# Rotary embedding on half of each head: cosine and sine rows landed on every fourth partition and gathered on VectorE

## The chip, the cores and the metric

The kernel runs on one core of one Trainium2 chip. The metric is the device time of the core in microseconds (us), lower is better; medians of several executions are given. All runs quoted here are at full granted clock. Profiles are of one execution; "span" is its length.

## The reference

```python
# x: 16 x 512 x 16 x 64 fp32;  cos, sin: 512 x 32 fp32
x1, x2 = x[..., :32], x[..., 32:]
a, b = x1[..., :16], x1[..., 16:]            # c, s: the first 16 columns of cos, sin by position
first  = a * c - b * s
second = a * s + b * c
out = concatenate([first, second, x2])       # 33.6 MB in, 33.6 MB out
```

## The kernel before

The 8192 positions are cut into four tiles of 128 partitions with 16 positions each (K = 16). Partition p of every tile needs rows 16(p mod 32) to 16(p mod 32)+15 of the tables, so a table of 32 partitions is replicated four times (REP = 4, PB = 32, Q = 16, HF = 32). A ring holds three tiles; each is loaded, rotated in place by VectorE and stored.

```python
ring  = const_pool.tile([P, NS, K, H, D], fp32)        # NS = 3
stage = const_pool.tile([PB, 2, K, HF], fp32)
table = const_pool.tile([P, 2, K, 2, Q], fp32)

nc.gpsimd.dma_start(out=stage[:, 0]..., in_=cosf)      # 64 KB each, issued by POOL
nc.gpsimd.dma_start(out=stage[:, 1]..., in_=sinf)
load(0, 0, K0); load(0, K0, K); load(1); load(2, 0, KC)  # issued by SP; K0 = 4, KC = 8
for r in range(REP):
    nc.vector.tensor_copy(out=table[r * PB : (r + 1) * PB]..., in_=stage[..., 0:Q] broadcast)

rotate(0, 0, K0); rotate(0, K0, 10); rotate(0, 10, K)  # four VectorE operations each
store(0)                                               # issued by SP too
load(2, KC, K)
load(3)                                                # needs tile 0's slot: waits for store(0)
for t in range(1, T):
    rotate(t, 0, KC); rotate(t, KC, K); store(t)
```

Of the kernel before, what the change touches and what calls it, by code (L numbers as in the profile page):

```python
# [1 line left out]

# [4 lines left out]


@with_exitstack
def kernel(  # L10
    ctx: ExitStack,
    tc: tile.TileContext,
    x: bass.AP,
    cos: bass.AP,
    sin: bass.AP,
    out: bass.AP,
):
    nc = tc.nc
    fp32 = mybir.dt.float32
    P = 128  # L20
    B, S, H, D = x.shape
    Q = D // 4
    HF = D // 2



    K = 16
    T = B * S // (P * K)
    PB = S // K
    REP = P // PB  # L30
    R = H * D
    NS = 3
    KC = K // 2
    K0 = K // 4

    xf = x.rearrange("b s h d -> (b s h d)").rearrange("(t p f) -> t p f", t=T, p=P)
    of = out.rearrange("b s h d -> (b s h d)").rearrange("(t p f) -> t p f", t=T, p=P)
    cosf = cos.rearrange("(p k) j -> p (k j)", k=K)
    sinf = sin.rearrange("(p k) j -> p (k j)", k=K)

    const_pool = ctx.enter_context(tc.tile_pool(name="const", bufs=1))
    b_pool = ctx.enter_context(tc.tile_pool(name="bp", bufs=1, space=bass.MemoryType.PSUM))


    ring = const_pool.tile([P, NS, K, H, D], fp32)
    stage = const_pool.tile([PB, 2, K, HF], fp32)
    table = const_pool.tile([P, 2, K, 2, Q], fp32)

    def rows(t, lo, hi):
        return ring[:, t % NS, lo:hi].rearrange("p k h d -> p (k h d)")  # L50

    def load(t, lo=0, hi=K):
        nc.sync.dma_start(out=rows(t, lo, hi), in_=xf[t, :, lo * R : hi * R])  # L53

    def store(t, lo=0, hi=K):
        nc.sync.dma_start(out=of[t, :, lo * R : hi * R], in_=rows(t, lo, hi))

    nc.gpsimd.dma_start(out=stage[:, 0].rearrange("p k j -> p (k j)"), in_=cosf)  # L58
    nc.gpsimd.dma_start(out=stage[:, 1].rearrange("p k j -> p (k j)"), in_=sinf)  # L59
    load(0, 0, K0)  # L60
    load(0, K0, K)
    load(1)
    load(2, 0, KC)


    for r in range(REP):
        nc.vector.tensor_copy(  # L67
            out=table[r * PB : (r + 1) * PB].rearrange("p t k c j -> p (t k) c j"),
            in_=stage.rearrange("p t k j -> p (t k) j")[:, :, 0:Q]
            .unsqueeze(2)  # L70
            .to_broadcast((PB, 2 * K, 2, Q)),
        )
    C = table[:, 0].rearrange("p k c j -> p k (c j)")
    Sn = table[:, 1].rearrange("p k c j -> p k (c j)")

    def rotate(t, lo, hi):
        n = hi - lo
        x1 = ring[:, t % NS, lo:hi, :, 0:HF]
        c = C[:, lo:hi].unsqueeze(2).to_broadcast((P, n, H, HF))
        s = Sn[:, lo:hi].unsqueeze(2).to_broadcast((P, n, H, HF))  # L80
        b_full = b_pool.tile([P, KC, H, HF], fp32, name="b_t")
        b_t = b_full[:, 0:n]
        nc.vector.tensor_mul(out=b_t, in0=x1, in1=s)  # L83
        nc.vector.tensor_mul(out=x1, in0=x1, in1=c)  # L84
        nc.vector.tensor_sub(  # L85
            out=x1[:, :, :, 0:Q], in0=x1[:, :, :, 0:Q], in1=b_t[:, :, :, Q:HF]
        )
        nc.vector.tensor_add(  # L88
            out=x1[:, :, :, Q:HF], in0=x1[:, :, :, Q:HF], in1=b_t[:, :, :, 0:Q]
        )  # L90

    rotate(0, 0, K0)
    rotate(0, K0, (K0 + K) // 2)
    rotate(0, (K0 + K) // 2, K)
    store(0)
    load(2, KC, K)
    load(3)
    for t in range(1, T):
        rotate(t, 0, KC)
        rotate(t, KC, K)  # L100
        store(t)


# [1 line left out]
_INS = ['x', 'cos', 'sin']  # L105
_OUTS = [((16, 512, 16, 64), 'float32')]


# [23 lines left out]
```

## Time and profile before

| | before |
|---|---|
| time | 161.92 us median of 6 (161.79 to 162.01) |
| span of the profiled run | 160.1 us |
| VectorE busy | 110.0 us, 69% |
| moved by DMA | 67.24 MB, 420 GB/s over the span |
| first rotation starts, second starts | 11.94 us, 23.66 us |
| first store issued | 44.14 us |

The prediction shows the slices, the stretches and the start of the timeline. One more view is needed later: three lines of the chain of waits of the kernel before. The columns are start, length, and what the chain went through.

```profile
1.17 22.39 DMA ring<-in_x_dram
...
44.14 28.18 DMA out_dram<-ring
72.34 28.75 DMA ring<-in_x_dram
```

These are the load of tile 0 (issued, until the whole tile is in), the store of tile 0, and the load of tile 3 into its slot. A transfer's length here is queueing and moving together: 28.18 us is not what 8.4 MB need (at the 433 GB/s of the middle stretches 19.4 us, an estimate), but what lay ahead of them in the queue as well. Between the load and the store the chain runs through VectorE's rotation of tile 0, 20.58 us here and in the changed kernel.

### The profile page before, as it was taken

To read this page: it belongs to the slowest core of one execution; us is meant where nothing else is said; L and a number is where in the kernel's file an instruction comes from. 1 tells how busy PE (TensorE), PEld (TensorE's weight loads), DVE (VectorE), ACT (ScalarE), POOL (GpSimd) and SP (SyncE) were. 2 spreads that over 40 slices of the span, in tenths; PEclk is the share of its full clock that TensorE was granted. 3 is DMA by queue.
4 is the path that set the end of the run, shared out by engine and by line. 5 is a ranking of instruction groups with operands and counts; after the bars stand their busy time and mean duration, and the time that the engine had idled before them with its cause. 6 is when DMAs were issued, how large, how long until landed. Compare 5 with 4: busy or idle time off the path is not lost.

```text
span 160.1 us, 109 instructions
## 1 busy us (share of the span) xinstructions
DVE 110.0 (69%) x40; POOL 1.3 (1%) x6
## 2 busy tenths in 40 slices
DVE  0069709999999999999999994799999900000000
POOL 3000000000000000000000000000000000000000
DMA  6999999699699799899996996996996996996991
GB/s 197 385 504 454 393 459 524 262 524 491 295 401 581 328 524 409 377 393 418 483 540 295 491 524 262 524 524 262 524 524 262 524 524 262 524 491 295 524 459 66
DMA packets 1504, 67.24 MB, mean 420 GB/s; under 512 B 192, under 2 KB 192, under 8 KB 224
## 3 DMA queue, kind: packets, MB, share of 16 engines
q1 hardware_dynamic: 1440, 67.11, 97.8%
q0 software_dynamic: 64, 0.13, 0.2%
HBM read 33.69 MB, written 33.55 MB: 420 GB/s over the span
## 4 chain that ended last, share of the span: by engine, by line
DMA 50%; DVE 28%; DVEq 1%; issue 0%; SPq 0%
DMA ring<-in_x_dram 32%; DMA out_dram<-ring 18%; DVE b_t L83 10%; DVE ring L84 10%; DVE ring L85 5%; DVE ring L88 3%; DVEq L127 1%; SPq L53 0%; DVEq L83 0%
## 5 line engine op out<-in xcount | busy, mean ns | idle before, releaser
L83 DVE TENSOR_TENSOR b_t<-ring,table 128x4096 f32<-128x4096 f32 (+2 forms) x9 | 35.6, 3959 | 8.2 <-DMA ring<-in_x_dram 8.0
L84 DVE TENSOR_TENSOR ring<-ring,table 128x4096 f32<-128x4096 f32 (+2 forms) x9 | 35.6, 3950 | 0.3
L85 DVE TENSOR_TENSOR ring<-ring,b_t 128x2048 f32<-128x2048 f32 (+2 forms) x9 | 18.4, 2049 | 0.3
L88 DVE TENSOR_TENSOR ring<-ring,b_t 128x2048 f32<-128x2048 f32 (+2 forms) x9 | 18.4, 2042 | 0.0
L67 DVE COPY table<-stage 32x1024 f32<-32x1024 f32 x4 | 2.7, 684 | 9.2 <-DMA stage<-in_sin_dram 9.1
L58 POOL DMA_DIRECT2D stage<-in_cos_dram x1 | 0.6, 631 | 0.8 <-PEq L127 0.8
L59 POOL DMA_DIRECT2D stage<-in_sin_dram x1 | 0.5, 498 | 0.0
L116 POOL MEMSET const-bfloat16-1.0<- 128x1 bf16 x1 | 0.1, 102 | 0.0
L116 POOL MEMSET const-float32-0.0<- 128x1 f32 x1 | 0.1, 99 | 0.2 <-issue 0.2
L116 POOL MEMSET const-float32-1.0<- 128x1 f32 x1 | 0.1, 99 | 0.0
L116 POOL MEMSET const-uint8-127<- 128x1 uint8 x1 | 0.1, 99 | 0.0
## 6 DMA issues: line engine op xcount, KB each, us to landing
ring<-in_x_dram SPq DMA_DIRECT2D x2, 4096.0 KB, 43.9
ring<-in_x_dram SPq DMA_DIRECT2D x1, 6144.0 KB, 22.4
ring<-in_x_dram SPq DMA_DIRECT2D x1, 2048.0 KB, 8.5
stage<-in_cos_dram POOLq DMA_DIRECT2D x1, 64.0 KB, 6.0
stage<-in_sin_dram POOLq DMA_DIRECT2D x1, 64.0 KB, 7.2
out_dram<-ring SPq DMA_DIRECT2D x4, 36.4
ring<-in_x_dram SPq DMA_DIRECT2D x2, 35.0
```

The lines of the kernel that those rows point to most:

```text
L58: nc.gpsimd.dma_start(out=stage[:, 0].rearrange("p k j -> p (k j)"), in_=cosf)
L59: nc.gpsimd.dma_start(out=stage[:, 1].rearrange("p k j -> p (k j)"), in_=sinf)
L67: nc.vector.tensor_copy(out=table[r * PB : (r + 1) * PB].rearrange("p t k c j -> p (t k) c j"), in_=stage.rearrange("p t k j -> p (t k) j" ...
L83: nc.vector.tensor_mul(out=b_t, in0=x1, in1=s)
L84: nc.vector.tensor_mul(out=x1, in0=x1, in1=c)
L85: nc.vector.tensor_sub(out=x1[:, :, :, 0:Q], in0=x1[:, :, :, 0:Q], in1=b_t[:, :, :, Q:HF])
L88: nc.vector.tensor_add(out=x1[:, :, :, Q:HF], in0=x1[:, :, :, Q:HF], in1=b_t[:, :, :, 0:Q])
L116: nc = _bacc.Bacc("TRN2", target_bir_lowering=False, num_devices=1)
L127: with _tile.TileContext(nc) as tc:
```

## The change

The likely intent is a quicker landing, with the rows on every fourth of 128 partitions instead of on 32 neighbouring ones. VectorE then brings them back to 32 partitions: the shuffle, with this mask, repeats within each group of 32 partitions that group's eight rows in order, and four copies, the widest first, leave rows 8q to 8q+7 of group q in their place; the result is right.

```diff
-    stage = const_pool.tile([PB, 2, K, HF], fp32)
+    stage = const_pool.tile([P, 2, K, HF], fp32)
+    spun = const_pool.tile([P, 2 * K, Q], fp32)
+    packed = const_pool.tile([PB, 2 * K, Q], fp32)
...
-    nc.gpsimd.dma_start(out=stage[:, 0].rearrange("p k j -> p (k j)"), in_=cosf)
-    nc.gpsimd.dma_start(out=stage[:, 1].rearrange("p k j -> p (k j)"), in_=sinf)
+    nc.vector.memset(stage[:, :, :, 0:Q], 0.0)
+    spread = stage.rearrange("(j b) t k i -> j b t (k i)", b=REP)
+    nc.gpsimd.dma_start(out=spread[:, 0, 0], in_=cosf)
+    nc.gpsimd.dma_start(out=spread[:, 0, 1], in_=sinf)
...
+    PQ = PB // REP
+    nc.vector.stream_shuffle(
+        out=spun[:],
+        in_=stage.rearrange("p t k j -> p (t k) j")[:, :, 0:Q],
+        mask=[j % PQ * REP for j in range(PB)],
+    )
+    for q in reversed(range(REP)):
+        n = PQ * (q + 1)
+        nc.vector.tensor_copy(out=packed[0:n], in_=spun[q * PB : q * PB + n])
     for r in range(REP):
         nc.vector.tensor_copy(
             out=table[r * PB : (r + 1) * PB].rearrange("p t k c j -> p (t k) c j"),
-            in_=stage.rearrange("p t k j -> p (t k) j")[:, :, 0:Q]
-            .unsqueeze(2)
-            .to_broadcast((PB, 2 * K, 2, Q)),
+            in_=packed.unsqueeze(2).to_broadcast((PB, 2 * K, 2, Q)),
         )
```

## The prediction

> **What bounds the kernel now.** I began with the page: the busy shares, then the slices, then the DMA queues.
>
> ```profile
> span 160.1 us, 109 instructions
> DVE 110.0 (69%) x40; POOL 1.3 (1%) x6
> ...
> DVE  0069709999999999999999994799999900000000
> POOL 3000000000000000000000000000000000000000
> DMA  6999999699699799899996996996996996996991
> ...
> q1 hardware_dynamic: 1440, 67.11, 97.8%
> q0 software_dynamic: 64, 0.13, 0.2%
> ```
>
> One slice is 4 us. The DMA row is nearly all nines from the second slice to the last but one; the sixes in it are large packets booked in the slice next door. VectorE is idle at the start, pauses twice, and does nothing for the last 32 us. The queue that carries x and the output is busy for 97.8% of 16 engines' span. The table queue is 0.2% of it: 0.002 x 160.1 = 0.3 us on each engine. So this looks bound by transfers, but a share over the span hides the stages. I therefore asked for stretches cut at the landmarks of the chain of waits (tile 0 in, tile 0 done, its store landed, tile 3 in, tile 3 done). Columns after the length: busy us of VectorE and of POOL with counts, TensorE clock, DMA share, GB/s.
>
> ```profile
> 0.00:24.00 24.00, 10.02 (x9) 1.33 (x6) 1.00 0.98 399
> 24.00:44.00 20.00, 19.83 (x8) 0.00 (x0) 1.00 0.97 419
> 44.00:72.00 28.00, 27.76 (x10) 0.00 (x0) 1.00 1.00 431
> 72.00:101.00 29.00, 25.72 (x8) 0.00 (x0) 1.00 1.05 452
> 101.00:128.00 27.00, 26.64 (x8) 0.00 (x0) 1.00 0.99 427
> 128.00:160.00 32.00, 0.04 (x1) 0.00 (x0) 1.00 0.91 393
> ```
>
> The four middle stretches move 20x419 + 28x431 + 29x452 + 27x427 = 45.1 MB in 104 us, 433 GB/s. At that rate the kernel's 67.24 MB need 155 us. The rest is the ends: the first 24 us move 9.6 MB where 433 GB/s would move 10.4 (2 us lost), the last 32 us move 12.6 MB where it would be 13.9 (3 us lost). 155 + 2 + 3 is the span. **The bound is the DMA engines, from first packet to last.**
>
> The change touches only the work ahead of the first rotation. So last I read the timeline there, start and length in us (the rotation's four instructions are lines 83, 84, 85, 88):
>
> ```profile
> 0.74 1.88 SPq L53 DMA_DIRECT2D ring<-in_x_dram  x4
> 1.25 0.63 POOL L58 DMA_DIRECT2D stage<-in_cos_dram  x1 [0.81 <-PEq L127]
> 1.88 0.50 POOL L59 DMA_DIRECT2D stage<-in_sin_dram  x1
> 9.13 2.77 DVE L67 COPY table<-stage 32x1024 f32<-32x1024 f32 x4 [9.13 <-DMA stage<-in_sin_dram]
> 11.94 2.30 DVE L83 TENSOR_TENSOR b_t<-ring,table 128x2048 f32<-128x2048 f32 x1
> ...
> 17.74 1.21 DVE L88 TENSOR_TENSOR ring<-ring,b_t 128x1024 f32<-128x1024 f32 x1
> 23.66 3.37 DVE L83 TENSOR_TENSOR b_t<-ring,table 128x3072 f32<-128x3072 f32 x1 [4.71 <-DMA ring<-in_x_dram]
> ```
>
> VectorE waits 9.13 us for the sine table, replicates it in 2.77 us, rotates the first quarter of tile 0, and is done at 18.95 us. Then it waits 4.71 us for the rest of tile 0. All four x loads are issued by SP from 0.74 us and wait for nothing on VectorE. The 4.71 us are **the first cushion**: a table that is ready up to 4.71 us later leaves the start of 23.66 us where it is.
>
> **A second and third cushion** lie in the DMA queue. When tile 0 is done (44.1 us) and its store is issued, 24x399 + 20x419 = 18.0 MB have moved of the 21.1 MB issued by then (loads of two and a half tiles of 8.39 MB, and the tables). So 3.1 MB, 7 us of work, are still queued: the store could come that much later without an idle DMA engine. When tile 3 is done (128.1 us), 67.2 - 12.6 = 54.6 MB have moved; of the 12.6 left the last store is 8.4, so 4.2 MB (about 10 us) are ahead of it.
>
> [...]in this trace a 64 KB table takes 6.0 and 7.2 us to land, nearly all of it not moving, as the 0.3 us per engine for both tables shows. [...]the tables land at about 9 us in the midst of x loads issued before them.
>
> [...]
>
> **The change part by part.** Nothing is removed; the four replications stay, reading another tile.
> - A memset of stage, 512 elements on 128 partitions. [...]The listing of the changed program has it first on VectorE, while VectorE has nothing else to do. But both table transfers overwrite stage, so POOL must wait for it. VectorE should start near 1.2 us, when POOL does now[...]
> - The scattered destination: the same 64 KB in 2 KB rows. 0 to -0.3 us for the landing; I count nothing.
> - The shuffle, 128x512:[...]
> - Four copies of 512 elements on 32, 24, 16 and 8 partitions. [...]
>
> The sum: 0.6 + 0.8 + 1.8 = **3.2 us later for the first rotation**, 15.1 instead of 11.94 us. It ends at 22.1, still before 23.66. The wait for tile 0 shrinks from 4.7 to 1.5 us and swallows all of it. On the path that sets the end: **0 us**. VectorE's busy time grows by 0.6 + 0.8 + 1.7 = 3.1 us, to 113.
>
> **The rivals.**
> - *The table becomes the bound of the start.* Should the memset, the shuffle or the landing cost 1.5 us more in sum than I reckoned, tile 0 starts late. For it: the shuffle is not measured here, and POOL's transfers take 6 to 7 us with causes I do not see in full. Against an effect: the second cushion of 7 us and the third of 10 are behind the first. Even a start 3 us later would leave the last store queued behind other bytes. Time: within 0.3 us of today.
> - *The scatter helps.* [...]spreading the rows could land the tables earlier and relieve the x loads beside them. For it: the first 24 us reach only 399 GB/s. Against it: much of that is the time before the first packet, and the tables are 0.13 of 67.24 MB. At most the tables' own 0.3 us per engine: 161.6.
> - *VectorE becomes the bound.* 113 of 160 us busy leaves it well short, and it idles for the last 32 us; no.
> - *Every VectorE microsecond counts, because it comes before the first store.* That would give 161.9 + 3.2 = 165.1, slower by 2.0%. It needs both the wait for tile 0 and the queued bytes to be illusions; the chain of waits passes through the load of tile 0, not through the table, so I hold it unlikely.
>
> **Range and chances.** The runs of before lie from 161.79 to 162.01 us. I expect 161.9. The range 161.3 to 162.5 covers that scatter, another chip, the 0.3 us of the helpful rival and half a microsecond for a start that slips. Faster by over 2% would need 3.2 us fewer of transfer: the bytes are the same, so 1%. Slower by over 2% needs the last rival in full: 2%. The rest is the same, 97%.
>
> **What would show it.** In the profile after: VectorE's memset ends near 1.8 us and POOL's first table issue moves from 1.25 to about 1.8 us; the sine wait ends near 9.7; shuffle near 0.78 us, copies near 0.42 each; the first rotation starts near 15; the second still starts near 23.7 with a wait of about 1.5 us on the x load ahead of it; the first store still near 44.1; the last near 128.1; DMA mean still 420 GB/s. The prediction is wrong if the wait ahead of the second rotation is gone and the end moves with it, or if the DMA rate of the middle stretches changes.

Cut from it is what rested on figures or rules that no trace of this case shows; with that go the grounds of every term of its sum. The sum came to 3.2 us for the first rotation: 0.6 for tables that are issued later because of the memset, 0.8 for the shuffle, 1.8 for the four copies. These were estimates. The trace of the kernel before has no memset on VectorE, no shuffle and no copy of 512 elements; its copies of 1024 elements on 32 partitions take 684 ns each. The changed kernel's trace then showed 0.485 us for the memset, 0.72 for the shuffle and 1.77 for the four copies.

## The result, and the profile after

The changed kernel takes **162.69 us** (162.55 to 162.87, 6 runs) against 161.92 (161.79 to 162.01, 6 runs). The ratio is 1.0048, 95% interval 1.0036 to 1.0061. (A ratio here is the mean time of one kernel's fast runs over that of the other's of the same rounds, so not quite the ratio of the medians.) That is within 2%, as expected, but 0.8 us slower and above the range.

First the page of the changed kernel: VectorE's and the DMA engines' rows by slice, and the data queue.

```profile
DVE 112.9 (70%) x47; POOL 1.4 (1%) x6
...
DVE  1049999999999999999999991699999900000000
...
DMA  6999999969999996999996996998998998998992
...
q1 hardware_dynamic: 1440, 67.11, 97.7%
```

The DMA row is as full as before, and VectorE's pause in the sixth slice is gone. Next, the start of its timeline (start, length, engine, line):

```profile
0.74 1.89 SPq L55 DMA_DIRECT2D ring<-in_x_dram  x4
0.92 0.48 DVE L61 MEMSET stage<- 128x512 f32 x1 [0.92 <-PEq L131]
1.71 0.65 POOL L63 DMA_DIRECT2D stage<-in_cos_dram  x1 [1.26 <-DVE stage L61]
...
10.14 0.01 DVE L74 LOAD_MASK_SELECT spun<-stage  x1 [8.74 <-DMA stage<-in_sin_dram]
10.17 0.72 DVE L74 STREAM_SHUFFLE spun<-stage 128x512 f32<-128x512 f32 x1
10.93 1.77 DVE L81 COPY packed<-spun 32x512 f32<-32x512 f32 x4
12.73 2.77 DVE L84 COPY table<-packed 32x1024 f32<-32x1024 f32 x4
15.54 2.30 DVE L98 TENSOR_TENSOR b_t<-ring,table 128x2048 f32<-128x2048 f32 x1
...
22.89 3.37 DVE L98 TENSOR_TENSOR b_t<-ring,table 128x3072 f32<-128x3072 f32 x1 [0.34 <-DMA ring<-in_x_dram]
```

VectorE's part went nearly as reckoned: the first rotation starts at 15.54 us, and what is left of the wait for tile 0 still covers all of it. The surprise is the last line: the second rotation starts at 22.89 us, **0.77 us earlier** than before. The chain of waits of the changed kernel goes on from there:

```profile
1.17 21.62 DMA ring<-in_x_dram
...
43.37 29.64 DMA out_dram<-ring
73.03 28.86 DMA ring<-in_x_dram
```

The load of tile 0 is 0.77 us shorter and the first store is issued 0.77 us earlier. But that store takes 29.64 us instead of 28.18: **1.46 us more**, though the same bytes lie ahead of it. The load of tile 3 adds 0.11. The sum, -0.77 + 1.46 + 0.11 = +0.80 us, is how much later tile 3 is in; the span of this execution is 0.87 us longer.

That this comes near the 0.77 us between the medians is partly luck. The profiled execution is the slowest of the six (162.87 us). The other five spans are 160.6 to 160.7 us, only 0.5 to 0.6 us above the 160.1 before. The rest, about 0.25 us, lies outside the span: there the changed kernel spends 1.93 to 2.14 us, the kernel before 1.8. That part belongs neither to the scatter nor to the stall described next: before_late_tables, before_longer_build and after_compact below have it too (2.05 us on average), though their spans are no longer than before. Its cause was not looked for and stays open.

Where in those 29.64 us? The trace has a record of every packet. Loads of half of tile 2 go in packets of 32 KB, nearly all of which take 1.213 to 1.222 us. In the changed kernel the last two such packets of every DMA engine (two rounds of 16), the very last before the store's, do not:

```
start of the last two 32 KB packets per engine, and their time
before    49.2 to 49.7 us: 1.21 to 1.22 us      50.4 to 51.0 us: 1.21 to 1.43 us
after     48.7 to 49.0 us: 1.90 to 2.36 us      50.8 to 51.4 us: 1.51 to 1.85 us
```

I call this **the stall**, and measure it as follows: for every packet of x or output that starts between the arrival of tile 1 and the arrival of half of tile 2, its time minus the usual one of its size (0.611, 1.213, 1.815, 2.418 us for 16, 32, 48, 64 KB), summed and divided by the 16 engines. Before: 0.09 us. After: 1.39 us. The same sum up to the arrival of tile 0 falls from 1.25 to 0.64 us, which is the gain at the start. Some 0.6 us of it lies in the first 4 us of both. The rest is 0.61 us before and 0.01 us after, and falls where the tables land: of the x packets that start between 4.5 and 9 us, 35 of 81 take 0.1 to 0.34 us too long before, and 1 of 82 after. The tables themselves are 32 packets of 4 KB in both kernels, so it is not their number that changed.

### The profile page after: what moved, and what is told of

Its sections match the earlier page's. It is cut to its first block, busy times and chain, and to the rows that moved or that the text cites. A ratio compares the mean times of both kernels' runs of the same rounds, so it can differ in the third digit from the quotient of the medians.

```text
span 160.9 us, 116 instructions
## 1 busy us (share of the span) xinstructions
DVE 112.9 (70%) x47; POOL 1.4 (1%) x6
## 3 DMA queue, kind: packets, MB, share of 16 engines
q1 hardware_dynamic: 1440, 67.11, 97.7%
HBM read 33.69 MB, written 33.55 MB: 418 GB/s over the span
## 4 chain that ended last, share of the span: by engine, by line
DMA 50%; DVE 28%; DVEq 1%; issue 0%; SPq 0%
DMA ring<-in_x_dram 31%; DMA out_dram<-ring 18%; DVE b_t L98 10%; DVE ring L99 10%; DVE ring L100 5%; DVE ring L103 3%; DVEq L142 1%; SPq L55 0%; DVEq L98 0%
## 5 line engine op out<-in xcount | busy, mean ns | idle before, releaser
L84 DVE COPY table<-packed 32x1024 f32<-32x1024 f32 x4 | 2.7, 684 | 0.1
L81 DVE COPY packed<-spun 32x512 f32<-32x512 f32 (+3 forms) x4 | 1.7, 416 | 0.1
L61 DVE MEMSET stage<- 128x512 f32 x1 | 0.5, 485 | 0.9 <-PEq L131 0.9
L74 DVE STREAM_SHUFFLE spun<-stage 128x512 f32<-128x512 f32 x1 | 0.7, 722 | 0.0
```

What stands on the lines that cost most here:

```text
L61: nc.vector.memset(stage[:, :, :, 0:Q], 0.0)
L74: nc.vector.stream_shuffle(out=spun[:], in_=stage.rearrange("p t k j -> p (t k) j")[:, :, 0:Q], mask=[j % PQ * REP for j in range(PB)],)
L81: nc.vector.tensor_copy(out=packed[0:n], in_=spun[q * PB : q * PB + n])
L84: nc.vector.tensor_copy(out=table[r * PB : (r + 1) * PB].rearrange("p t k c j -> p (t k) c j"), in_=packed.unsqueeze(2).to_broadcast((PB, ...
```

## The experiments

Two things had to be explained: why a landing place of 0.13 MB makes the load of 8.4 MB beside it 0.7 us faster, and why the first change from loads to stores, 30 us later, then costs 1.3 us. Each kernel was run in at least four executions beside the kernel before on the same chip; the stall and the arrivals are from one trace each.

### First round: which part of the change

**after_again.** The changed kernel, unedited.

> The changed kernel once more, for a second trace. In its first trace all 16 DMA engines needed about 1 us longer at the end of the load of half of tile 2, where the first store follows (packets of 32 KB that take 1.21 us elsewhere took 1.9 to 2.4 us). If that stall belongs to the kernel (theory A: the change shifts how the DMA engines stand to each other when loads turn into stores), it is there again and the time is again 162.5 to 162.9 us against 161.9. If it is an event of one profile (theory B), this trace does not have it, the time is still about 162.7, and the 0.8 us have to be found elsewhere.

162.73 us against 162.09, ratio 1.0044 (1.0030 to 1.0057). The stall is there again: 1.28 us, in the same two rounds of packets. It belongs to the kernel.

**before_late_tables.** The kernel before with the memset alone.

```diff
-    stage = const_pool.tile([PB, 2, K, HF], fp32)
+    stage_all = const_pool.tile([P, 2, K, HF], fp32)
+    stage = stage_all[0:PB]
+    nc.vector.memset(stage_all[:, :, :, 0:Q], 0.0)      # ahead of the two table transfers
```

> The kernel before with only the memset ahead of the table transfers, so that they are issued about 0.5 us later and land later; no scatter, no shuffle. If the later tables alone shift the DMA engines against each other: 162.4 to 162.9 us. If the scatter or VectorE's later start does it: 161.8 to 162.0 us.

162.16 us, ratio 1.0007 (0.9994 to 1.0021). The first rotation starts at 13.38 instead of 11.94 us and it does not matter. The memset is not the cause.

**before_longer_build.** The kernel before with useless work between landing and first rotation.

```diff
+    nc.vector.stream_shuffle(out=spun[0:PB], in_=stage..., mask=list(range(PB)))
+    for q in reversed(range(REP)):
+        n = PQ * (q + 1)
+        nc.vector.tensor_copy(out=packed[0:n], in_=spun[0:n])     # nobody reads packed
```

> The kernel before with only VectorE's work made longer: a shuffle and four copies on 32 partitions into tiles that nobody reads, about 2.5 us, after tables that are issued and land as before. If the later first rotation costs something: 162.4 us or more. If the wait for the rest of tile 0 swallows it, as the prediction had it: 161.8 to 162.0 us.

162.31 us, ratio 1.0009 (0.9995 to 1.0022). The wait for tile 0 swallows the work, as the prediction had it.

**after_compact.** The changed kernel with the rows landing on partitions 0 to 31 again; memset, shuffle and copies stay.

```diff
-    spread = stage.rearrange("(j b) t k i -> j b t (k i)", b=REP)
+    near = stage[0:PB].rearrange("p t k i -> p t (k i)")
-        mask=[j % PQ * REP for j in range(PB)],
+        mask=list(range(PB)),
-        nc.vector.tensor_copy(out=packed[0:n], in_=spun[q * PB : q * PB + n])
+        nc.vector.tensor_copy(out=packed[0:n], in_=spun[0:n])
```

> The changed kernel with only the scatter undone: the tables land on partitions 0 to 31, memset, shuffle (identity) and copies stay, and the result stays right. If the scattered landing causes the loss: back to 161.8 to 162.0 us. If memset or VectorE's work does: 162.4 to 162.9 us as the changed kernel.

162.33 us, ratio 1.0006 (0.9992 to 1.0020). VectorE executes the same operations as in the changed kernel; its first rotation starts even later, at 16.14 us. The three lines of its chain are those of the kernel before:

```profile
1.16 22.58 DMA ring<-in_x_dram
...
44.32 28.23 DMA out_dram<-ring
72.57 28.77 DMA ring<-in_x_dram
```

So neither VectorE's work nor the memset makes the loss. The landing place does.

### Second round: the landing place alone

**scatter_only.** The kernel before with the scattered landing and nothing else. VectorE waits for both transfers by copying one partition (0.41 us, from 8.35 us on, when the sine is in); the tables are zero elsewhere, so the result is wrong.

```diff
+    nc.gpsimd.dma_start(out=spread[:, 0, 0], in_=cosf)   # stage on 128 partitions, no memset
+    nc.gpsimd.dma_start(out=spread[:, 0, 1], in_=sinf)
+    nc.vector.tensor_copy(out=base[0:1], in_=stage...[0:1, :, 0:Q])
-            in_=stage... broadcast
+            in_=base.unsqueeze(2).to_broadcast((PB, 2 * K, 2, Q)),
```

> The kernel before with the tables landing on every fourth partition and nothing else of the change: no memset ahead of them, no shuffle, no gathering copies (the tables built are mostly zero, so the result is wrong on purpose). If the scatter alone is the cause: x of tile 0 is in about 0.7 us earlier than before (22.4 instead of 23.1 us), the last load ahead of the first store loses about 1.3 us, and the time is 162.5 to 162.9 us. If the scatter needs the memset's delay beside it: 161.9 to 162.1 us or, with the gain at the start and no loss, about 161.4 us.

162.74 us against 161.88, ratio 1.0056 (1.0043 to 1.0069), stall 1.26 us:

```profile
1.18 21.56 DMA ring<-in_x_dram
...
43.32 29.49 DMA out_dram<-ring
72.82 28.75 DMA ring<-in_x_dram
```

Both halves of the effect, the shorter load and the longer store, come from the scatter alone.

**every_second.** The changed kernel with the rows on every second of 64 partitions; two copies gather them.

```diff
-    stage = const_pool.tile([P, 2, K, HF], fp32)
+    stage = const_pool.tile([2 * PB, 2, K, HF], fp32)    # spun likewise
-    spread = stage.rearrange("(j b) t k i -> j b t (k i)", b=REP)
+    spread = stage.rearrange("(j b) t k i -> j b t (k i)", b=2)
-    PQ = PB // REP                                       # and REP -> 2 in mask and loop
+    PQ = PB // 2
```

> The changed kernel with the rows on every second partition (64 partitions[...]), two gathering copies instead of four, result right. [...]as the kernel before, 161.9 to 162.3 us, tile 0 in at about 23.1 us. If any strided landing does it: as the changed kernel, 162.5 to 162.9 us, tile 0 in at about 22.4 us.

(The first outcome was foreseen if what counts is not the stride but over how many partitions the rows are spread. Why 64 should do as 32 do was the author's guess, and is cut.)

162.07 us, ratio 1.0010 (0.9998 to 1.0022), stall 0.04 us:

```profile
1.17 22.43 DMA ring<-in_x_dram
...
44.17 28.21 DMA out_dram<-ring
```

The landing is strided as in the change, but the x load and the store are those of the kernel before. So it is not the stride. With the rows spread over 64 partitions the load of tile 0 takes 22.43 us, as with 32 (22.39 before, 22.58 in after_compact); with 128 it takes 21.62. Why, no run shows.

**after_reload.** The changed kernel, which after the shuffle loads both tables once more onto partitions 0 to 31, to no use.

```diff
+    nc.gpsimd.dma_start(out=stage[0:PB, 0].rearrange("p k j -> p (k j)"), in_=cosf)
+    nc.gpsimd.dma_start(out=stage[0:PB, 1].rearrange("p k j -> p (k j)"), in_=sinf)
```

> The changed kernel, and after the shuffle both tables are loaded once more onto partitions 0 to 31, to no use, only to disturb the DMA engines as the kernel before did: 0.13 MB, 0.3 us for each engine. If the loss at the change from loads to stores comes from how the engines stand to each other (theory A): the stall of 1.3 us at 48.7 us is gone or far smaller, and in spite of the extra bytes the time is 162.0 to 162.3 us, below the changed kernel's 162.7. If the stall comes from where the tables lie or from VectorE's order (theory B), it stays and the time is about 163.0 us.

The stall is gone: 0.04 us, and the first store takes 28.20 us. But the second load itself makes tile 0 arrive 1.24 us later (23.64 us instead of 22.40), more than expected, so the time is 162.68 us (ratio 1.0046, 1.0034 to 1.0058), no better. I had expected 162.0 to 162.3. The mechanism half of the expectation held, the sum did not.

**before_reload.** The control: the same two lines in the kernel before.

> The control: the kernel before with the same useless second load of both tables on partitions 0 to 31 after the replications. It says what the extra load costs by itself: 0.3 us or so, 162.2 to 162.5 us, no stall at the change from loads to stores.

162.57 us, ratio 1.0046 (1.0033 to 1.0058), no stall (0.09 us). So a second landing of 0.13 MB on partitions 0 to 31 costs 0.7 us by itself, more than the 0.3 us that its bytes take. (The trace is of its fastest execution, 162.27 us, and shows only half of that: tile 0 in at 23.37 us instead of 23.10.)

### Third round: other landing places, and none

**upper_rows.** The kernel before with the tables on partitions 64 to 95.

```diff
+    stage_all = const_pool.tile([P, 2, K, HF], fp32)
+    stage = stage_all[64 : 64 + PB]
```

> The kernel before with the tables on partitions 64 to 95[...]; result right, nothing else changed. [...]no stall at the first change from loads to stores, tile 0 in at about 23.1 us, 161.8 to 162.1 us. If partitions 0 to 31 themselves matter: 162.5 us or more.

(The first outcome was foreseen if it does not matter which 32 neighbouring partitions the rows land on.)

162.14 us, ratio 1.0020 (1.0006 to 1.0034), tile 0 in at 22.99 us, stall 0.30 us. Nearly as the kernel before; the small stall that it does have was not expected.

**no_tables.** The kernel before without the two transfers; the tables are a constant, the result is wrong.

```diff
-    nc.gpsimd.dma_start(out=stage[:, 0]..., in_=cosf)
-    nc.gpsimd.dma_start(out=stage[:, 1]..., in_=sinf)
+    nc.vector.memset(base[:], 0.5)
-            in_=stage... broadcast
+            in_=base.unsqueeze(2).to_broadcast((PB, 2 * K, 2, Q)),
```

> The kernel before without the two table transfers: the tables are a constant, the result is wrong on purpose. [...]Theory C, engines in step stall at the change from loads to stores: tile 0 in at about 22 us, a stall of 1 us or more at about 48 us, and 162.0 to 162.5 us, no faster than before although two transfers are gone. Rival, the scattered landing itself sets off the stall: no stall, 161.0 us or less.

161.99 us, ratio 1.0005 (0.9993 to 1.0017). **Taking the two transfers away gains nothing**:

```profile
1.16 21.29 DMA ring<-in_x_dram
...
43.03 29.44 DMA out_dram<-ring
```

The load of tile 0 is 1.10 us shorter than before, and the stall (1.27 us) takes it back. So the scattered landing does not set off the stall; the stall is what the stream of loads meets here with no tables beside it, and the landing on partitions 0 to 31 of the kernel before had been keeping it away (0.09 us there, 0.08 in after_compact).

**cos_scattered.** Half of the change: the cosine on every fourth partition, the sine on 0 to 31.

```diff
+    nc.vector.memset(stage_c[:, :, 0:Q], 0.0)
+    nc.gpsimd.dma_start(out=spread[:, 0], in_=cosf)                      # every fourth partition
+    nc.gpsimd.dma_start(out=stage_s.rearrange("p k j -> p (k j)"), in_=sinf)  # 0 to 31
+    # shuffle, gathering copies for the cosine only; 8 replications of 512 elements
```

> Half of the change: the cosine on every fourth partition with its memset, shuffle and copies, the sine on partitions 0 to 31; result right. If the push that the engines get at the start sets the size of the stall: tile 0 in at about 22.7 us, a stall between 0.1 and 1.3 us. With less than 0.4 us of stall it would beat both kernels: 161.6 us. With the full stall: 162.8 us.

162.35 us, ratio 1.0028 (1.0017 to 1.0040), tile 0 in at 22.73 us, stall 0.72 us: half the change, half of both effects.

**split_halves.** The kernel before with the cosine on partitions 0 to 31 and the sine on 64 to 95.

```diff
+    nc.gpsimd.dma_start(out=stage_c[0:PB]..., in_=cosf)
+    nc.gpsimd.dma_start(out=stage_s[64 : 64 + PB]..., in_=sinf)
```

> The kernel before with the cosine on partitions 0 to 31 and the sine on 64 to 95: [...]result right. Theory C, [...]the stall is there, about 1 us, 162.3 to 162.9 us. [...]no stall, 161.8 to 162.1 us.

(The stall was foreseen if theory C holds, no stall if each landing on 32 neighbouring partitions is enough by itself.)

162.38 us, ratio 1.0028 (1.0015 to 1.0041), stall 0.59 us. Neither of the two expectations: it lies between. The spans, 160.0 to 160.4 us against 160.0 to 160.3 in the same round, are no longer: the later store (stall +0.5 us) is nearly paid by the earlier load (tile 0 in at 22.72 us, -0.4), and the 0.45 us of time lie outside the span. It decides for neither.

### Fourth round: the moment, or the state of the stream

Over these runs the stall was the larger the earlier tile 1 had arrived. That left a rival: something at a fixed time, which only early streams run into.

**late_start.** The changed kernel with all x loads held back by a small memset.

```diff
+    nc.vector.memset(ring[:, :, K0 - 1 : KC + 1, 0, 0:16], 0.0)    # every first load overlaps it
     load(0, 0, K0)
```

> The changed kernel with every x load made to wait for a small memset on VectorE, so that the stream starts about 0.9 to 1.1 us later; tables, shuffle and copies stay, the result stays right. Over all twelve runs the stall at the first change from loads to stores is the larger the earlier tile 1 is in (1.3 us where it is in at 41.4 to 41.8 us, 0.6 us at 42.1, 0 to 0.1 us at 42.5 or later). If the moment is what counts (theory T): tile 1 is in at about 42.7 us, the stall is gone, and a later start costs nothing or gains: 161.9 to 162.3 us. If the engines' order among themselves counts (theory C): the stall stays at 1.3 us and the delay is added, 163.5 to 163.8 us.

163.73 us, ratio 1.0112 (1.0098 to 1.0126). The loads start 0.99 us later, tile 1 is in at 42.81 us, later than before's 42.46, and the stall is still 1.24 us:

```profile
2.15 21.70 DMA ring<-in_x_dram
...
44.43 29.30 DMA out_dram<-ring
```

The rival of the moment falls.

**no_tables_late_start.** The same memset, a little larger, in the kernel without tables (result wrong).

> The kernel without table transfers (constant tables, result wrong on purpose), with the same late start of the x loads, about 1 us. Theory T: tile 1 in at 42.4 us or later, stall gone or under 0.3 us, 161.8 to 162.1 us, no slower than with the early start (161.99). Theory C: nothing has been done to the engines' order, stall 1.3 us, 162.9 to 163.1 us.

163.25 us, ratio 1.0080 (1.0066 to 1.0094), stall 1.32 us: again the delay is simply added.

**after_load2_whole and before_load2_whole.** Both kernels with tile 2 loaded in one piece ahead of the first store.

```diff
-    load(2, 0, KC)
+    load(2)
...
-    load(2, KC, K)
```

> The changed kernel with tile 2 loaded in one piece ahead of the first store, so that the first change from loads to stores comes 9.7 us later and with 64 KB packets. If the stall belongs to that change: it moves to about 60 us or vanishes; nothing happens at 48 to 51 us. If it belongs to the moment, some event at about 49 us whatever is in flight: packets slow there all the same. Time: 161.3 us if it vanishes without another cost (faster than both kernels), about 162.7 if it moves along.

> The control: the kernel before with tile 2 loaded in one piece ahead of the first store. Without a stall of its own it stays at 161.7 to 162.1 us.

171.51 us after, 170.77 before (ratios 1.0586, 1.0570 to 1.0601, and 1.0553, 1.0533 to 1.0573). Both are far slower for a reason of their own, which I had not foreseen: the DMA engines run dry (by my reading because the load of tile 3 is issued too late), two slices of 4.2 us in which the row of the kernel before with this edit is zero:

```profile
DMA  5988995999699989988998899799969950099955
```

For the stall they answer the question all the same. After: packets starting at 58 us are 1.27 us too long per engine, and none from 45 to 57 us. Before: 0.06 us at 58 and 59 us. The stall moved 10 us along with the first store's packets, and the two kernels still differ by 0.7 us.

**after_act_stores and before_act_stores.** Stores issued by ACT on a queue of their own (q10 of the page, 33.55 MB, beside q1's 33.55), so that loads no longer queue with the stores.

```diff
-        nc.sync.dma_start(out=of[t, :, lo * R : hi * R], in_=rows(t, lo, hi))
+        nc.scalar.dma_start(out=of[t, :, lo * R : hi * R], in_=rows(t, lo, hi))
```

> The changed kernel with its stores issued by ACT on a queue of their own[...]. If the stall needs a clean change from loads to stores with the engines in step: no packets 0.7 us or more too long at one moment, and the gain of the scatter at the start (0.7 us) remains: 160.5 to 161.5 us, faster than the same edit of the kernel before by 0.3 to 0.7 us. If loads and stores side by side cost as much by themselves, or the order of the loads gets worse: 162.5 us or more.

> The control: the kernel before with its stores issued by ACT. 161.0 to 162.0 us if a queue of their own costs nothing; above the changed kernel's by 0.3 to 0.7 us if the scatter's gain at the start remains there.

181.25 us after, 180.56 before (ratios 1.1195, 1.1180 to 1.1211, and 1.1154, 1.1138 to 1.1169). A miss as an improvement: VectorE waits up to 25 us for a load, and again the engines run dry, for four slices of 4.5 us in both. And the expectation that the stall would vanish failed too: packets that start from 44 to 47 us, just after the first store is issued at 43.5 us and in the midst of loads, are 1.2 us too long per engine after, 0.17 before. So the stall needs no last load; it comes in the load packets just ahead of the first store's, the first of which starts at 48.5 us.

### All traces side by side

Worked out from the packet records, one trace per run. Columns: arrival of tile 1 counted from the first packet; packet time above the usual, per engine, up to the arrival of tile 0; the stall.

```
                        tile 1 in   above usual, start   stall
no_tables_late_start      39.66 us         0.54 us       1.32 us
no_tables                 39.70            0.58          1.27
scatter_only              39.94            0.60          1.26
after                     39.97            0.64          1.39
after_again               40.00            0.60          1.28
late_start                40.09            0.62          1.24
cos_scattered             40.32            0.76          0.72
split_halves              40.32            0.82          0.59
before_longer_build       40.43            1.02          0.39
before_late_tables        40.45            1.02          0.20
upper_rows                40.61            0.99          0.30
before                    40.71            1.25          0.09
every_second              40.73            1.27          0.04
after_compact             40.82            1.25          0.08
before_reload             40.97            1.33          0.09
after_reload              41.27            1.48          0.04
```

In these traces, the more the stream of loads was held up at the start, the smaller the stall. The exchange is a bad one: from 1.25 to 0.6 us the hold-up saves 0.65 us, and the stall costs 1.2. The net of 0.55 us is what the spans show: +0.4 to +0.6 us on average for the changed kernel, after_again and scatter_only. No run beat the kernel before. At the second change from loads to stores (packets that start from 97 to 102 us) the same sum is 0.06 us before and 0.25 after.

One trace each is little. The same landing place held the loads up by 1.25 us in the trace of before and by 1.02 to 1.08 in four others (before_longer_build, before_late_tables, before_load2_whole, before_act_stores), with tile 0 in at 23.10 and at 22.85 to 22.89 us. So differences of 0.2 us in these columns are not to be explained.

What stays open is what inside the DMA engines carries the hold-up of the first 10 us (or, in after_reload, of 16 to 22 us) forward to the first store. It is not simply how far the engines have drifted apart: tile 1 arrives on the 16 engines within 0.26 us in the changed kernel and 0.48 us in no_tables, both with the stall, and within 0.50 us before and 0.30 us in before_reload, both without. The records do not name a packet's engine, so a finer order could not be read. Theory C of the expectations (engines in step stall, engines out of step do not) is therefore not shown; shown is that what was done to the stream at its start sets the stall, and that the moment does not.

## Why the prediction was wrong

- *VectorE's part* was right. Memset 0.485 us (0.6 foreseen), POOL's first issue at 1.71 us (1.8), shuffle 0.72 us with 0.01 for its mask (0.78), copies 414 to 420 ns each, on 32 partitions as on 8 (0.42 us foreseen), VectorE busy 112.9 us (113), first rotation at 15.54 us (15.1). The sine landed at about 10.1 us instead of 9.7, and at 8.5 in the second trace; it is not a fixed number.
- *The first cushion* held: before_late_tables and before_longer_build spend part of it each and stay at ratios of 1.0007 and 1.0009. That the wait shrank to 0.34 instead of 1.5 us is the later sine and the earlier load.
- *The second and third cushion* were not tested: in no run did VectorE start tile 0 late because of its tables. But the data queue was as full in the changed kernel (97.7% against 97.8%), and it is still slower: a full queue does not mean a stream of constant length.
- *The rival "the scatter helps"* had the right sign at the start and the wrong size. I bounded it by "the tables' own 0.3 us per engine". Measured: tile 0 in at 23.10 us before, 22.40 scattered, 22.09 without tables. The scattered tables cost the x loads just their 0.3 us, those on partitions 0 to 31 1.0 (0.8 in four other traces). The bound left out what such a landing does to the transfers beside it: the 35 of 81 x packets that take 0.1 to 0.34 us too long.
- **The step that failed** is in the part on the bound and in the change part by part: "The scattered destination: the same 64 KB in 2 KB rows. 0 to -0.3 us for the landing; I count nothing", with the sum "On the path that sets the end: 0 us". I took the length of the x and output stream as given by its bytes and 433 GB/s. In its place the runs show a stream whose length depends on its start: -0.77 us for the load of tile 0, +1.46 us for the first store, +0.11 for the load of tile 3. These are the sizes of one trace, the slowest execution; in the spans of the other five 0.5 to 0.6 us of it remain, and about 0.25 us of the time lie outside the span. The range, half a microsecond each way, had no room for that.
- The test that I named, "the DMA rate of the middle stretches changes", was the right one: from 44 to 72 us the kernel before moved 431 GB/s, the changed one 413.

```profile
44.00:72.00 28.00, 27.79 (x9) 0.00 (x0) 1.00 1.00 413
```

That line is the changed kernel's; the DMA share, 1.00 in both, shows no difference, because a packet that takes longer counts as busy. Only the bytes show it.

## What to carry to other kernels

In a kernel whose DMA engines are always busy, follow the lengths of single transfers in the chain of waits, not the busy share: here 1.39 us per engine were lost inside busy packets, at a share of 1.00. A small transfer can cost the large ones beside it more than its bytes (here 0.13 MB on partitions 0 to 31 cost 0.8 to 1.0 us instead of 0.3, on every fourth of 128 partitions 0.3), so look at where it lands. Compare spans as well as times: here a third of the loss, and in split_halves all of it, lay where no trace reaches. And test a "cleaner" start by its effect on the end: here even removing the disturbing transfers altogether gained nothing, since the first store took back what the loads had won.
